# Hybrid decoder layer on one core: the first three heads of cross attention's first half in written order on all engines

## The chip, the core and the metric

The kernel runs on one core of a Trainium2 chip. The metric is device time in microseconds (us). The core has a matrix engine (TensorE, PE in the profile), three engines for the rest (VectorE is DVE, ScalarE is ACT, GpSimd is POOL), each with an instruction queue of its own that is worked off in order, and a queue (SyncE, SP) that issues the transfers between the main memory and the core's buffers. Engines wait for each other through semaphores. Matrix products are gathered in eight banks of PSUM.

## The reference

One decoder layer, 1024 tokens of 1024 columns, in float32: two mixers in parallel (mLSTM and forgetting attention), then cross attention over 256 memory tokens in four heads of 256 columns, then an MLP with squared ReLU, each behind an RMS norm.

```python
def cross_attention(h, memn, w_q, w_kv, w_o):
    q = (h @ w_q).reshape(B, S, X_HEADS, X_DH)
    k, v = jnp.split(memn @ w_kv, 2, axis=-1)
    ...
    s = jnp.einsum('bqhd,bmhd->bhqm', q, k) * (X_DH ** -0.5)
    p = jax.nn.softmax(s, axis=-1)
    o = jnp.einsum('bhqm,bmhd->bqhd', p, v).reshape(B, S, D)
    return o @ w_o
```

The change lies in the queries, scores, softmax and values of this function.

## The kernel before

Every float32 operand is split into a high half (rounded to the engine's fast format, ScalarE, line 134 or 137) and a low half (what is left over, VectorE, line 135 or 138). `mm3` multiplies them in three matmuls, lines 186 (low weight by high operand), 187 (high by low) and 188 (high by high). What is called a cut below is such a split.

The 1024 tokens are worked in two halves of 512. For the **first half** of cross attention each head has two query tiles (`n` = 0 to 7 over the four heads). A tile takes a weight load of 512 KB (`weights`, two buffers `wr` for the raw weights and three pairs `wh`, `wl` for the halves), eight times three matmuls into a PSUM bank (`mm` for the even tile, `m2` for the odd one; each exists once; the profile calls the second `m`), and a cut that also evicts it, into `r_b`, `r_c` or `r_p`, `r_a`, `r_y`. `cross_head` then does, for one head: loads of keys and values; scores of four token tiles into two of three `sc` banks; the maximum (line 1289, times `rcol` in 1291) on VectorE, four exponentials on ScalarE (1293), a reciprocal (1294), four scalings (1296); a `yield`; eight transposes on PE (1301, the turns) into two `tp` banks and the cut of these (`r_d`, `r_e`); two value products, one for each 128 columns of the head, each gathered in the one `ov` bank and cut into `oh`, `ol` (both `act` tiles).

For the **second half** the queries are made another way: `query_blocks` multiplies blocks of the weights, added and subtracted beforehand (`left_query`: SP loads two raw tiles at once, VectorE line 1223 and GpSimd lines 1339 and 1227 add, cuts follow), by seven combinations of the normed tokens (`R`, made by `right_side(k)` for k = 0 to 3, tiles also called `act`). `right_side(k)` loads two tiles into the two `r_f` buffers, scales them (ScalarE, 1177), cuts three pieces, and then three times subtracts on GpSimd (1339) in place and cuts the result. A product of `query_blocks` sums over all four k.

`row_second(1)` makes the second half's norm factors: `rsqrt_sums` sums columns on PE (234) into `ov`, VectorE, GpSimd (a power, 204) and VectorE again make `rcol`; `to_row` turns it on PE (249), copies it (ScalarE, 250) and sends it by way of main memory into `row`.

What sets the order: the kernel is recorded in the order of the Python code, and then a scheduler with its own picture of times orders each engine's queue, by dependencies and by what it takes to be ready. Only inside `in_order()` are the instructions of PE, ScalarE, VectorE and GpSimd (not SP) tied to the written order; instructions written outside such a block may still be placed between them. In the kernel before, the loop over the four heads of the first half lies outside any such block, so the scheduler lays products of later tiles and of `query_blocks` between a head's steps.

Of the kernel before, what the change touches and what calls it, by code (L numbers as in the profile page):

```python
# [21 lines left out]
KT = D // P  # L22
# [22 lines left out]
def hybrid_layer(ctx: ExitStack, tc: tile.TileContext, a: dict, out: bass.AP):  # L45
# [123 lines left out]
    def weights(src, n=1024):  # L169
        return weight_parts(weight_load(src, n))  # L170
# [992 lines left out]
    def cut_right(c, k, x):  # L1163
        split(R[c][0][:, k], R[c][1][:, k], x)

    fourth = []

    def right_side(k):
        if not fourth:
            for c in (("11", "21"), ("t1", "t2"), ("22", "t3")):  # L1170
                right_room(*c)
            fourth.append(w4((P, 4, 256)))
        x, y = w2("f"), w2("f")
        for t, n in ((x, k), (y, 4 + k)):
            with tc.issue_after(mix_done[0].ins):
                load(t, x1d[1, :, n])
            s.activation(t, t, AF.Copy, scale=ln_x(n))
# [12 lines left out]
    def q_room(kk):  # L1190
        return [rotate(*tags).bitcast(F32R) for tags in ((("b",), ("c",)), (("p",), ("a", "y")))[kk]]

    def query_whole(hd):
        q = []
        for kk in range(2):
            t = q_room(kk)
            for _, _, ps in proj(weights(a["w_xq"][2 * hd + kk]), [h2], 1, order=[(0, 0)], into=ps_tile(("mm", "m2")[kk])):
                split(*t, ps, 1.0 / 16.0)
            q.append(t)
        return q  # L1200

    x_jobs = [(hd, i) for hd in range(XH) for i in X_ORDER]
    x_first = {}
# [69 lines left out]
    def cross_head(hd, hf, q, oh, ol):  # L1273
        kx, vx = w4(dt=F32R), w4(dt=F32R)
        with tc.issue_after(mix_done[0].ins):
            load(kx.bitcast(F32), kxd[hd].rearrange("p e k c -> p (e k c)"))
            load(vx.bitcast(F32), vxd[hd].rearrange("p e m c -> p (e m c)"))
        kx, vx = (t.rearrange("p (e k c) -> p e k c", e=2, k=2) for t in (kx, vx))
        vx_parts = (vx[:, 0], vx[:, 1])
        pts = [(w2("d", dt=F32R), w2("e", dt=F32R)) for _ in range(2)]  # L1280
        pr = z4()[:, :T].rearrange("p (i c) -> p i c", i=4)
        den, rden, mxc = col("den", 4), col("rden", 4), col("mx", 4)
        sps = [sc().rearrange("p (i c) -> p i c", i=2) for _ in range(2)]
        for i in range(4):
            sp = sps[i // 2]
            for kk in range(2):
                mm3(sp[:, i % 2], both(q[kk], lambda z: z[:, i * P : (i + 1) * P]), (kx[:, 0, kk], kx[:, 1, kk]), kk == 0, kk == 1)
            if i % 2:
                v.tensor_reduce(out=mxc[:, i - 1 : i + 1], in_=sp, axis=mybir.AxisListType.X, op=ALU.max, negate=True)

                v.tensor_tensor(out=mxc[:, i - 1 : i + 1], in0=mxc[:, i - 1 : i + 1], in1=rcol[:, 4 * hf + i - 1 : 4 * hf + i + 1], op=ALU.mult)
        for i in range(4):
            s.activation(pr[:, i], sps[i // 2][:, i % 2], AF.Exp, bias=mxc[:, i : i + 1], scale=rcol[:, 4 * hf + i : 4 * hf + i + 1], accum_out=den[:, i : i + 1])
        v.reciprocal(rden, den)
        for i in range(4):
            s.activation(pr[:, i], pr[:, i], AF.Copy, scale=rden[:, i : i + 1])
        yield
        for m in range(2):
            ps = tp()
            for i in range(4):  # L1300
                nc.tensor.transpose(ps[:, i * P : (i + 1) * P], pr[:, i, m * P : (m + 1) * P], ident)
# [36 lines left out]
    def sub(out_, x, y, by=v):  # L1338
        by.tensor_tensor(out=out_, in0=x, in1=y, op=ALU.subtract)
# [108 lines left out]
    os_ = []  # L1448
    whole = act(), act()
    os_.append([Rows(enumerate(t[:, n] for n in range(KT))) for t in whole])  # L1450
    for hd in range(XH):
        q = query_whole(hd)
        right_side(hd)
        if hd == XH - 1:
            last_room = right_room("t4")
            for k in range(4):
                cut_right("t4", k, fourth[0][:, k])
            for _ in range(2):
                left_query(*x_prep.pop(0))
# [388 lines left out]
```

## Time and profile before

| | |
|---|---|
| time, median of 3 runs | 1511.72 us (1510.87 to 1512.04) |
| span of the profiled execution | 1509.2 us |
| instructions | 22358 |
| TensorE's mean granted clock | 0.997 |
| the stage of the change in the trace | from about 628 us |

The span runs from the first to the last instruction of the profiled execution; the timed runs are some 2.5 us longer, with what lies around it. The profile has no other time of that execution. A row of a timeline gives the start in us from the span's start, the duration in us, the engine, the line, the operation, the tile written and the tiles read (without buffer numbers), the shape, the count of equal instructions that follow each other, and in brackets the idle time of the engine before it with what ended that. PE's matmuls overlap: the next starts before the last has ended, so a PE that is busy all the time can still run slower than it could, and the distance from start to start is what counts.

### The profile page before, as it was taken

What the parts mean: (1) busy time and instruction counts of PE and PEld (TensorE: products, weight loads), DVE (VectorE), ACT (ScalarE), POOL (GpSimd) and SP (SyncE); (2) the same over time, 40 slices, a digit from 0 to 9 for tenths busy, and PEclk for the clock granted to TensorE, in tenths of its full rate; (3) what the DMA queues carried; (4) which work ended last, traced back from release to release, by engine and by line L of the source; (5) the groups of instructions that cost most, each with busy time, mean ns of one, the idle gap of its engine ahead of it and who ended that gap; (6) DMA issues with size and microseconds to landing.
All of it is one profiled execution on the core that took longest, in us unless ns stands there. A gap on an engine that the chain in (4) does not pass through costs nothing.

```text
span 1509.2 us, 22358 instructions
## 1 busy us (share of the span) xinstructions
PE 1493.0 (99%) x7806; PEld 1263.7 (84%) x7806; DVE 1122.7 (74%) x1803; ACT 757.7 (50%) x1440; POOL 528.7 (35%) x545
## 2 busy tenths in 40 slices
PE   9999999999999999999999999999999999999997
PEld 9988888889899888788988878888888888888887
DVE  7766676664788875667767899989996678787765
ACT  7324343334688764566654467566664521122134
POOL 1003030414365441623300044454544365553312
PEclk9999999999999999999999999999999999999999
DMA  6322333435777877853354447676678677776623
GB/s 243 115 79 95 98 108 126 132 129 153 247 261 256 284 248 246 271 169 126 128 182 159 147 155 279 235 261 248 217 273 292 264 279 279 279 272 251 247 88 112
DMA packets 124276, 303.04 MB, mean 201 GB/s; under 512 B 13810, under 2 KB 28460, under 8 KB 117252
## 3 DMA queue, kind: packets, MB, share of 16 engines
q1 hardware_dynamic: 124164, 301.62, 57.3%
q8 instruction: 61, 1.00, 0.3%
q14 instruction: 51, 0.42, 0.1%
HBM read 202.75 MB, written 98.82 MB: 200 GB/s over the span
## 4 chain that ended last, share of the span: by engine, by line
PE 90%; DMA 4%; DVE 3%; ACT 1%; issue 1%; POOL 1%; POOLq 0%; DVEq 0%; SPq 0%; ACTq 0%
PE tp L186 8%; PE tp L187 8%; PE tp L188 8%; PE sc L186 6%; PE sc L188 6%; PE sc L187 6%; PE mm L186 5%; PE m L188 5%; PE m L186 5%; PE m L187 5%; PE mm L188 5%; PE mm L187 5%; PE ov L801 2%; PE ov L186 2%; PE ov L187 2%; PE ov L188 2%
## 5 line engine op out<-in xcount | busy, mean ns | idle before, releaser
L186 PE MATMUL tp<-act,wl 128*128 128x512 f32 (+1 forms) x440 | 172.6, 392 | 0.0
L187 PE MATMUL tp<-act,wh 128*128 128x512 f32 (+1 forms) x440 | 172.1, 391 | 0.0
L188 PE MATMUL tp<-act,wh 128*128 128x512 f32 (+1 forms) x440 | 171.8, 392 | 0.0
L135 DVE TENSOR_TENSOR wl<-wr,wh 128x1024 fp32r<-128x1024 f32 (+2 forms) x99 | 131.4, 1327 | 27.0 <-ACT wh L134 26.7
L134 ACT ACTIVATE wh<-wr 128x1024 fp32r<-128x1024 f32 (+2 forms) x99 | 99.8, 1008 | 85.7 <-PE tp L188 32.7
L186 PE MATMUL mm<-act,wl 128*128 128x512 f32 (+1 forms) x332 | 124.8, 376 | 2.6 <-DVE r_c L138 2.1
L188 PE MATMUL mm<-act,wh 128*128 128x512 f32 (+1 forms) x332 | 124.1, 374 | 0.0
L187 PE MATMUL mm<-act,wh 128*128 128x512 f32 (+1 forms) x332 | 123.8, 373 | 0.0
L186 PE MATMUL m<-act,wl 128*128 128x512 f32 (+1 forms) x308 | 113.8, 369 | 0.6 <-DVE wl L135 0.6
L188 PE MATMUL m<-act,wh 128*128 128x512 f32 (+1 forms) x308 | 113.8, 369 | 0.0
L187 PE MATMUL m<-act,wh 128*128 128x512 f32 (+1 forms) x308 | 113.7, 369 | 0.0
L188 PE MATMUL sc<-act,wh 128*128 128x512 f32 (+1 forms) x280 | 105.6, 377 | 0.0
L187 PE MATMUL sc<-act,wh 128*128 128x512 f32 (+1 forms) x280 | 105.6, 377 | 0.0
L186 PE MATMUL sc<-act,wl 128*128 128x512 f32 (+1 forms) x280 | 105.6, 377 | 0.0
L1612 POOL TENSOR_TENSOR z<-wr 128x256 f32<-128x256 f32 x56 | 52.9, 966 | 131.8 <-DMA wr<-w_ff2q 126.7
L188 PEld LDWEIGHTS tp<-act,wh 128*128 128x128 f32 x440 | 82.7, 188 | 19.0
L186 PEld LDWEIGHTS tp<-act,wl 128*128 128x128 f32 x440 | 82.7, 188 | 18.5
L187 PEld LDWEIGHTS tp<-act,wh 128*128 128x128 f32 x440 | 82.7, 188 | 18.2
L134 ACT ACTIVATE wh<-z 128x1024 fp32r<-128x1024 f32 (+1 forms) x54 | 55.5, 1027 | 81.8 <-POOL z L1612 62.3
L135 DVE TENSOR_TENSOR wl<-z,wh 128x1024 fp32r<-128x1024 f32 (+1 forms) x54 | 77.7, 1439 | 11.4 <-ACT wh L134 11.4
L134 ACT ACTIVATE w<-wr 128x768 fp32r<-128x768 f32 (+3 forms) x35 | 28.0, 801 | 107.4 <-PE tp L186 33.0
L186 PEld LDWEIGHTS mm<-act,wl 128*128 128x128 f32 x332 | 62.7, 189 | 14.2 <-DVE r_c L138 2.6
(734 smaller groups left out, 4387.2 us busy)
## 6 DMA issues: line engine op xcount, KB each, us to landing
act<-right SPq DMA_DIRECT2D x49, 1024.0 KB
right<-w SPq DMA_DIRECT2D x56, 256.0 KB
wr<-w_ff2q SPq DMA_DIRECT2D x28, 512.0 KB
right<-r_d SPq DMA_DIRECT2D x49, 256.0 KB
right<-r_e SPq DMA_DIRECT2D x49, 256.0 KB
act<-fqk SPq DMA_DIRECT2D x48, 256.0 KB
wr<-w_in SPq DMA_DIRECT2D x20, 512.0 KB
wr<-w_ff SPq DMA_DIRECT2D x20, 512.0 KB
```

What stands on the lines that cost most here:

```text
L134: s.activation(hi, src, AF.Copy)
L135: return v.tensor_tensor(out=lo, in0=src, in1=hi.bitcast(F32), op=ALU.subtract)
L186: nc.tensor.matmul(ps, w[1], x[0], start=first, stop=False, skip_group_check=more)
L187: nc.tensor.matmul(ps, w[0], x[1], start=False, stop=False, skip_group_check=more)
L188: nc.tensor.matmul(ps, w[0], x[0], start=False, stop=last, skip_group_check=more)
L801: nc.tensor.matmul(self.ov[:, c0:], self.fv[:, self.j], t[:, c0:], start=self.j == 0 and t is self.p[1], stop=self.last and t is self.p[0])
L1612: g.tensor_tensor(out=o, in0=x, in1=y, op=op)
```

## The change

The loop over the first three heads is put inside `in_order()`. The query tiles are made one at a time by three small functions (weights, product, cut), and a head's steps stand so: the cut of the next head's first tile, scores and softmax, the product of the next head's second tile, the first part of `right_steps`, the turns, the cut of that tile, the product of the tile after it, the rest of `right_steps`, another weight cut, the values. `row_second(1)` moves from behind head 0 to between the first two products and the third. Head 3 stays outside, and its two query tiles are made by then. `right_side` becomes a generator with one `yield`, and `cross_head` gets a second `yield` between turns and values.

```diff
+    def right_steps(k):
...
         cut_right("11", k, x1)
         cut_right("21", k, y1)
         cut_right("22", k, y2)
+        yield
         sub(x1, x2, x1, g)
         cut_right("t1", k, x1)
...
-    def query_whole(hd):
...
+    w_query, p_query, queries = {}, {}, {}
+
+    def query_weights(n):
+        if n < KT:
+            w_query[n] = weights(a["w_xq"][n])
+
+    def query_product(n):
+        if n < KT:
+            ((_, _, p_query[n]),) = proj(w_query.pop(n), [h2], 1, order=[(0, 0)], into=ps_tile(("mm", "m2")[n % 2]))
+
+    def query_cut(n):
+        if n < KT:
+            queries[n] = q_room(n % 2)
+            split(*queries[n], p_query.pop(n), 1.0 / 16.0)
...
             split(*pts[m], ps)
+        yield
         for kk in range(2):
...
-    for hd in range(XH):
-        q = query_whole(hd)
-        right_side(hd)
-        if hd == XH - 1:
...
-        for _ in cross_head(hd, 0, q, *os_[0]):
-            pass
-        if hd == 0:
-            row_second(1)
+    with in_order():
+        for n in range(2):
+            query_weights(n)
+        query_product(0)
+        query_weights(2)
+        query_cut(0)
+        query_product(1)
+        row_second(1)
+        query_weights(3)
+        query_cut(1)
+        query_product(2)
+        for hd in range(XH - 1):
+            query_cut(2 * hd + 2)
+            query_weights(2 * hd + 4)
+            steps = cross_head(hd, 0, [queries.pop(2 * hd + kk) for kk in range(2)], *os_[0])
+            next(steps)
+            query_product(2 * hd + 3)
+            side = right_steps(hd)
+            next(side)
+            next(steps)
+            query_cut(2 * hd + 3)
+            query_product(2 * hd + 4)
+            next(side, None)
+            query_weights(2 * hd + 5)
+            for _ in steps:
+                pass
+    right_side(XH - 1)
...
+    for _ in cross_head(XH - 1, 0, [queries.pop(2 * XH - 2 + kk) for kk in range(2)], *os_[0]):
+        pass
```

How the queues stand at three places, before and after. Line numbers of the changed kernel are some 4 to 11 higher (1181 for 1177, 1307 for 1296, 1312 for 1301, 1351 for 1339).

First, ScalarE where head 0's queries are evicted (`mm_7130` and `m_1357` are the first two tiles; `act_7192` to `act_7194` hold the right side). Before:

```order
L222 ACTIVATE r_c_7106<-r_p_7102 128x512
L134 ACTIVATE act_7192<-r_f_7197 128x256
L134 ACTIVATE act_7194<-r_f_7197 128x256
L134 ACTIVATE act_7193<-r_f_7196 128x256
L134 ACTIVATE act_7194<-r_f_7196 128x256
L137 ACTIVATE r_b_7122<-mm_7130 128x512
L134 ACTIVATE wh_7358<-wr_7356 128x1024
```

After (`mm_7134`, `m_1358` and `mm_7222` are the first three tiles, `ov_7207` the turned norm factors):

```order
L222 ACTIVATE r_c_7106<-r_p_7102 128x512
L137 ACTIVATE r_b_7165<-mm_7134 128x512
L250 ACTIVATE row<-ov_7207 8x128
L134 ACTIVATE wh_7214<-wr_7212 128x1024
L137 ACTIVATE r_p_7218<-m_1358_7169 128x512
L137 ACTIVATE r_b_7247<-mm_7222 128x512
L134 ACTIVATE wh_7253<-wr_7251 128x1024
```

The right side's cuts, which wait for GpSimd, have moved from ahead of the first query eviction to behind head 0's softmax.

Second, PE where head 0's values are made (`ov_7283` and `ov_7292` before, `ov_7408` and `ov_7417` after). Before, the first value product:

```order
L187 MATMUL sc_7424<-w_1399_7411,r_b_7319 128x256
L186 MATMUL ov_7283<-r_d_7222,w_1365_7219 128x512
L188 MATMUL sc_7424<-w_1399_7411,r_b_7319 128x256
...
L187 MATMUL ov_7283<-r_e_7225,w_1365_7219 128x512
L188 MATMUL ov_7283<-r_d_7224,w_1365_7219 128x512
L186 MATMUL m_1426_7537<-act_6784,wl_7534 128x512
```

After, from the last matmul of a query product on:

```order
L188 MATMUL mm_7367<-act_6784,wh_7253 128x512
L186 MATMUL ov_7408<-r_d_7261,w_1376_7258 128x512
...
L187 MATMUL ov_7408<-r_e_7264,w_1376_7258 128x512
L188 MATMUL ov_7408<-r_d_7263,w_1376_7258 128x512
L186 MATMUL ov_7417<-r_d_7261,w_1376_7258 128x512
...
L188 MATMUL ov_7417<-r_d_7263,w_1376_7258 128x512
L186 MATMUL sc_7448<-w_1409_7436,r_c_7248 128x256
```

Before, head 1's scores and a query product of 24 matmuls and more stood between the two value products; now the second follows the first in the same bank.

Third, head 2 between its softmax and its values. ScalarE before (`z_1435` holds the probabilities, `tp_7637` the first turns, `act_7761` the fourth right tile):

```order
L1296 ACTIVATE z_1435_7594<-z_1435_7594,c_rden_7596 128x256 x4
L134 ACTIVATE act_7761<-w_1361_7195 128x256 x4
L137 ACTIVATE r_p_7704<-m_1456_7712 128x512
L134 ACTIVATE wh_7879<-wr_7772 128x1024
...
L134 ACTIVATE r_d_7590<-tp_7637 128x512
```

ScalarE after (`z_1442` the probabilities, `r_f_7681` and `r_f_7682` the right side's slice 2, `tp_7693` and `tp_7700` the turns):

```order
L1307 ACTIVATE z_1442_7613<-z_1442_7613,c_rden_7615 128x256 x4
L1181 ACTIVATE r_f_7681<-r_f_7681,vec 128x512
L1181 ACTIVATE r_f_7682<-r_f_7682,vec 128x512
L134 ACTIVATE act_7761<-w_1391_7336 128x256 x2
L134 ACTIVATE wh_7879<-wr_7772 128x1024
L134 ACTIVATE act_7333<-r_f_7681 128x256
L134 ACTIVATE act_7333<-r_f_7682 128x256
L134 ACTIVATE act_7335<-r_f_7682 128x256
L134 ACTIVATE r_d_7609<-tp_7693 128x512
L134 ACTIVATE r_d_7611<-tp_7700 128x512
L137 ACTIVATE r_p_7707<-m_1448_7656 128x512
```

PE after, from the second tile of turns on (`mm_7883` is the first block of `query_blocks`, its matmuls here read slice 2; `sc_7802` are head 3's scores):

```order
L1312 MATMUL tp_7700<-ident,z_1442_7613 128x128 x4
L186 MATMUL mm_7883<-act_7333,wl_7778 128x256
L186 MATMUL ov_7721<-r_d_7609,w_1437_7606 128x512
L187 MATMUL mm_7883<-act_7333,wh_7777 128x256
L188 MATMUL mm_7883<-act_7333,wh_7777 128x256
L187 MATMUL ov_7721<-r_e_7610,w_1437_7606 128x512
...
L187 MATMUL ov_7721<-r_e_7612,w_1437_7606 128x512
L188 MATMUL ov_7721<-r_d_7611,w_1437_7606 128x512
L186 MATMUL sc_7802<-w_1467_7790,r_y_7708 128x256
```

Before, the right side had been cut long ahead of this place and other products stood around the turns; now slice 2 of the right side is cut between softmax and turns, and on PE only pieces that read this slice or the turns stand there.

More of the change, by code (lines that the diff above doesn't have):

```diff
@@ L1450, in hybrid_layer @@
     os_.append([Rows(enumerate(t[:, n] for n in range(KT))) for t in whole])
-    for hd in range(XH):
-        q = query_whole(hd)
-        right_side(hd)
-        if hd == XH - 1:
[L1455 to L1459, printed above, removed]
-        for _ in cross_head(hd, 0, q, *os_[0]):
-            pass
-        if hd == 0:
-            row_second(1)
+    with in_order():
[25 more added lines that the diff above has]
+    right_side(XH - 1)
+    last_room = right_room("t4")
+    for k in range(4):
+        cut_right("t4", k, fourth[0][:, k])
+    for _ in range(2):
+        left_query(*x_prep.pop(0))
+    for _ in cross_head(XH - 1, 0, [queries.pop(2 * XH - 2 + kk) for kk in range(2)], *os_[0]):
+        pass
     oh, ol = Rows(), Rows()
```

8 lines of the change are left out of this document (1 added, 7 removed).

## The prediction

> **What bounds the kernel now.** I read the page first: the busy shares and the chain of waits.
>
> ```profile
> span 1509.2 us, 22358 instructions
> PE 1493.0 (99%) x7806; PEld 1263.7 (84%) x7806; DVE 1122.7 (74%) x1803; ACT 757.7 (50%) x1440; POOL 528.7 (35%) x545
> PE 90%; DMA 4%; DVE 3%; ACT 1%; issue 1%; POOL 1%; POOLq 0%; DVEq 0%; SPq 0%; ACTq 0%
> ```
>
> TensorE (PE) is busy for 99% of the span and is 90% of the chain that ended last. So the change, which moves no arithmetic, can only win the time in which PE waits or runs slowly, and whatever new wait it gives PE is paid in full. Next come the stretches of the edited stage (us; then busy time and instructions of PE, PEld, DVE, ACT and POOL; granted clock; DMA share; GB/s), and PE's own timeline at the two places where it is not dense.
>
> ```profile
> 628.16:639.20 11.04, 11.04 (x49) 8.92 (x49) 5.57 (x10) 4.89 (x9) 7.05 (x7) 1.00 0.85 281
> 639.20:642.46 3.26, 1.12 (x5) 0.63 (x4) 2.94 (x4) 2.71 (x7) 2.03 (x3) 1.00 0.63 250
> 642.46:645.88 3.42, 3.42 (x11) 2.65 (x10) 2.59 (x4) 2.10 (x4) 0.00 (x0) 0.50 0.87 287
> 645.88:704.60 58.72, 58.72 (x346) 50.70 (x346) 38.02 (x71) 39.23 (x95) 16.95 (x18) 1.00 0.43 139
> ```
>
> ```profile
> 638.97 0.40 PE L187 MATMUL m<-act,wh 128*128 128x512 f32 x1
> 639.20 0.39 PE L188 MATMUL m<-act,wh 128*128 128x512 f32 x1
> 641.74 0.50 PE L186 MATMUL mm<-act,wl 128*128 128x512 f32 x1 [2.14 <-DVE r_c L138]
> 642.60 0.63 PE L186 MATMUL mm<-act,wl 128*128 128x512 f32 x1
> 643.03 0.63 PE L187 MATMUL mm<-act,wh 128*128 128x512 f32 x1
> ...
> 704.53 0.28 PE L187 MATMUL sc<-act,wh 128*128 128x256 f32 x1
> 704.65 0.28 PE L188 MATMUL sc<-act,wh 128*128 128x256 f32 x1
> 705.34 0.38 PE L186 MATMUL mm<-act,wl 128*128 128x256 f32 x1 [0.42 <-DVE wl L135]
> ```
>
> Starts follow each other by 0.23 us at 512 columns and by 0.12 at 256, so a query tile's product (24 matmuls) is 5.6 us of PE, a head's scores (24 of 256) 2.86, one value product (6 of 512) 1.4.
>
> **What goes.** After 639.20 the next start is 2.54 us later instead of 0.23: 2.3 lost. For the next 3.42 us the clock is 0.50 and the pitch 0.43: eight matmuls lose about 0.2 each, 1.65 with the edges. At 704.65 another 0.57 is lost. Together 4.5 us. The first wait is the one that the new order on ScalarE removes: the query eviction stood behind cuts that waited for GpSimd.
>
> ```profile
> 639.74 0.42 ACT L134 ACTIVATE act<-r_f 128x256 fp32r<-128x256 f32 x1 [0.53 <-POOL r_f L1339]
> 640.18 0.60 ACT L137 ACTIVATE r_b<-mm 128x512 fp32r<-128x512 f32 x1
> 641.01 0.68 DVE L138 SCALAR_TENSOR_TENSOR r_c<-mm,r_b 128x512 fp32r<-128x512 f32 x1
> ```
>
> The tile had been finished since about 634; now its eviction runs during the next product and is free, as that product covers it by over 4 us.
>
> **What comes, a: the row of the second norm.** `row_second(1)` now stands between products 1 and 2 on PE: sums, a chain over VectorE and GpSimd, then a transpose that reads its result. Nothing on PE may pass. The kernel's end has the same chain:
>
> ```profile
> 1499.04 1.31 PE L1748 MATMUL sc<-ones,r_b 128*128 128x1 f32 x8 [0.49 <-POOL r_b L226]
> 1500.63 0.71 POOL L1750 TENSOR_TENSOR c_y<-c_var,half 128x2 f32<-128x2 f32 x1 [1.64 <-DVE c_var L1749]
> 1501.97 0.71 PE L213 MATMUL mm<-ident,c_r 128*128 128x128 f32 x4 [1.62 <-DVE c_r L1754]
> ...
> 633.28 1.02 POOL L204 TENSOR_TENSOR c_y<-c_var,half 128x4 f32<-128x4 f32 x1
> ```
>
> PE idles 1.62 there; four columns instead of two make GpSimd 0.3 longer: 1.9, I take **2.0**. Behind the transpose on PE stands product 2, then head 0's scores, so all of the stage moves. The sums and the transpose themselves are not new, they ran later.
>
> **b: one bank for two value products.** The `ov` bank exists once. In heads 0 and 1 the second product now follows the first, so PE waits for the whole split. In the profile other matmuls stood between.
>
> ```profile
> 696.71 0.39 PE L188 MATMUL ov<-r_d,w 128*128 128x512 f32 x1
> 697.13 0.60 ACT L134 ACTIVATE act<-ov 128x512 fp32r<-128x512 f32 x1 [2.37 <-PE ov L188]
> 698.35 0.68 DVE L135 TENSOR_TENSOR act<-ov,act 128x512 fp32r<-128x512 f32 x1
> ```
>
> End of PE to ScalarE 0.03, then 0.60, hop 0.04, 0.68, hop 0.05: idle 1.40, and 1.57 from start to start. The split also queues behind the right side's three cuts and a weight cut, written ahead of it. Counted from the end of the turns, PE is through the first value product after 5.6 + 1.4 = 7.0. In head 0 that queue ends at 6.7 on ScalarE and 7.9 on VectorE, so the low half of the split is ready at 8.6: **1.6**. In head 1, where the turns come late (c), VectorE is through at 8.8 and the low half at 9.4: **2.4**. Behind it stand the second value product and the next head's scores.
>
> **c: head 1's turns.** The loads are in no written order, but SP issues them one after the other, and each waits for its buffer there. Weights 3 to 7 and the keys of heads 1 and 2 are issued over 5 us before their use, so I cost them at nothing; ahead of that cover only a load slower by 5 us would show. One load is late. Ahead of the scaling of the probabilities ScalarE now holds a cut of the second half's first weight tile, and VectorE an add on it. That load needs the buffer of tile 6, whose cut ends 3.4 us after the scores' start, and loads take 3.5:
>
> ```profile
> 691.45 0.33 SPq L174 DMA_DIRECT2D wr<-w_xq  x1
> 695.01 0.70 DVE L1223 TENSOR_TENSOR wr<-wr 128x512 f32<-128x512 f32 x1 [2.61 <-DMA wr<-w_xq]
> 658.89 1.69 ACT L1296 ACTIVATE z<-z,c_rden 128x256 f32<-128x256 f32 x4
> 728.82 1.03 PE L1301 MATMUL tp<-ident,z 128*128 128x128 f32 x8
> ```
>
> Landing at 7.0, add and reciprocal to 7.95, scaling to 9.65; PE, with scores and one product, is there at 8.46, and its eight turns end at 10.25 instead of 9.36: **0.9**. In head 0 the chain has half a us to spare.
>
> **d: head 2, turns to values.** In heads 0 and 1 a query product lies between turns and values; head 2 has none (no tile 8). After the last scaling, ScalarE holds two gains, two cuts of the fourth tile, a weight cut and three right cuts before it evicts the turns; VectorE the same halves.
>
> ```profile
> L1177 ACT ACTIVATE r_f<-r_f,vec 128x512 f32<-128x512 f32 x8 | 5.8, 724 | 9.8 <-DMA r_f<-x1d 9.8
> L134 ACT ACTIVATE wh<-wr 128x1024 fp32r<-128x1024 f32 x15 | 15.9, 1058 | 2.5 <-DMA wr<-w_xq 1.2 <-POOL wr L1227 1.2
> 656.14 1.22 DVE L135 TENSOR_TENSOR wl<-wr,wh 128x1024 fp32r<-128x1024 f32 x1 [0.26 <-ACT wh L134]
> 660.49 1.02 ACT L134 ACTIVATE act<-r_f 128x256 fp32r<-128x256 f32 x3
> 682.89 1.28 DVE L135 TENSOR_TENSOR r_e<-tp,r_d 128x512 fp32r<-128x512 f32 x2
> ```
>
> From the last scaling: gains 1.26, cuts 0.65, weight high half 1.05 (to 2.95), VectorE's low half 1.22 (4.2), three low cuts (5.3), two turn halves 1.28 (6.55), the last query cut (7.1), which head 3's scores need. PE ends the turns at 0.5 and has nine matmuls (1.76) in these 6.6 us: **4.9**.
>
> **e: head 3 and the first query block.** The last slice of the right side loads into a buffer that head 2's third sum frees, at about 10.0 on the same clock (three GpSimd steps of 0.85 with the cuts between).
>
> ```profile
> 664.71 0.85 POOL L1339 TENSOR_TENSOR r_f<-r_f,r_f 128x256 f32<-128x256 f32 x1 [1.55 <-DVE act L135]
> 666.41 0.80 SPq L1176 DMA_DIRECT2D r_f<-x1d  x2
> 669.83 0.73 ACT L1177 ACTIVATE r_f<-r_f,vec 128x512 f32<-128x512 f32 x1 [3.81 <-DMA r_f<-x1d]
> L1293 ACT ACTIVATE z<-sc,c_mx,rcol 128x256 f32<-128x256 f32 x20 | 11.1, 560 | 4.1 <-DVE c_var L198 3.3 <-DVE c_mx L1291 0.8
> ```
>
> Issue to use is 3.3, so 13.3. Then ScalarE alone has 8.6 us (two gains, four exponentials, six cuts of 0.31, one of 0.52, one eviction, four scalings, a turn), and with VectorE's half head 3's values start at 22.3. PE has 5.05 us of scores, block parts and values ready from 7.1 on (18 score matmuls 2.15, twelve of the block 1.45, a value product 1.4) and 2.7 more in pieces behind the cuts (three times three of the block, the eight turns, half a value product): 15.2 less 7.75 is **7.4**. No product of the block can step in, since each sums over all four slices of the right side and the last slice is the late one. From there on the block has all it needs, and I count nothing.
>
> **The clock.** Each wait long enough may cost a stretch at half clock, 1.65. In the rows above an idle 2.14 did it; this one of 1.07 did not:
>
> ```profile
> 385.44 0.50 PE L734 MATMUL sc<-act 128*128 128x512 f32 x1 [1.07 <-ACT act L756]
> 385.44:392.00 6.56, 6.56 (x52) 6.39 (x53) 5.39 (x18) 4.15 (x12) 3.67 (x6) 1.00 1.01 358
> ```
>
> Five new waits (a, b of head 1, d, two in e) lie near or over 2: none to five stretches, 0 to 8.3; I take two, **3.3**, as the waits of d and e are partly empty time where a slow clock harms nothing.
>
> The Trainium skill, page "TensorE: Matmul & The Clock Gate", section "HAM oscillation — how this bites in real kernels", sets the rule at no idle gap over about 3.4 us. The row of 2.14 goes against it as a bound on one gap. By the page only d and e could slow the clock, and the sum would be 1.65 lower.
>
> **The sum.** 2.0 + 1.6 + 0.9 + 2.4 + 4.9 + 7.4 + 3.3 = 22.5, less 4.5: 18.0 us over the profiled span, 1527.2. The median shown, 1511.72, is 2.5 above the span; I carry that over: 1529.7, say **1529**, 1.1% slower. Moving values ahead adds no PE work: all these matmuls ran before, later.
>
> **Unknowns.** d and e rest on chains of ten and more steps; if loads land a us earlier and half of d and e is covered, 6.2 go, without slow clocks 3.3 more: 1520. All five stretches and VectorE's weight half at its crowded mean (1.34 for 1.22) give 1536; a block that starves after that, 1538.
>
> **Rivals.**
> - *Only the order's two fixed waits count.* a and twice b, 5.2, against 4.5 gone, perhaps one slow stretch: 1512.4 to 1514.1, **1513**. It needs ScalarE in heads 2 and 3 to keep up; for it, ACT is busy 39 of 58.7 us in the fourth stretch above. Against it, the last head has no product to hide 6.6 us of queue. Chance 0.12, two thirds of it inside 0.2%.
> - *Faster.* The starved places fill with block products that need only the slices already cut, and the bank is handed over within another product's tail. 4.5 goes and 1.0 comes: **1508**. It decides at a to e together under 1.5 us. The fixed orders of PE at a and b alone speak against it. Chance 0.04.
> - *The clock as the bound.* PE works in pieces from head 1 to the first block, stays at 0.50 for most of it and pays over 9: **1540**. For it, one wait of 2.14 was enough; against it, dense stretches in between. Chance 0.06.
>
> My forecast keeps 0.78. Slower by over 0.2% (3 us, about what a measurement can tell from no change): 0.78 + 0.06 + 0.04 = 0.88; within: 0.08; faster: 0.04. The range 1513 to 1538 takes in the first rival's middle.
>
> **What the profile after would show.** No wait of `mm` on the first query cut; about 2.0 idle before the transpose of `rcol`; `ov` waiting for VectorE's `act` half twice, about 1.4 and 2.2; PE waiting before head 2's `ov` and head 3's scores, some 5 in all; PE before the block's `mm` and `m` on ScalarE's right cuts, some 7; several stretches of clock 0.50. I am wrong if PE stays dense from head 2's turns on, or if the loads of the right side's last slice start before head 2's cuts end.

## The result and the profile after

| | before | after |
|---|---|---|
| time, median of 4 runs each | 1511.3 us (1509.7 to 1512.0) | 1536.5 us (1534.0 to 1537.7) |
| span of the profiled execution | 1509.2 us | 1534.8 us |
| mean granted clock | 0.997 | 0.991 |

The ratio is 1.0161, with a 95% interval of 1.0148 to 1.0173: slower by 25 us. The forecast was slower, 1529, in a range of 1513 to 1538. The direction and the range held; the size was 7.5 us short, and the measured time lies 1.5 us below the upper end of a range 25 us wide. Where the record has both, a timed run lies some 1.7 us above its own span; the 2.5 carried over in the prediction is that and some 0.8 by which the profiled execution was faster than the median.

First the page of the changed kernel: span, busy time of PE, and the chain that ended last.

```profile
span 1534.8 us, 22367 instructions
PE 1503.5 (98%) x7806; PEld 1268.3 (83%) x7806; DVE 1125.4 (73%) x1803; ACT 758.2 (49%) x1440; POOL 528.1 (34%) x545
PE 89%; DVE 4%; DMA 3%; ACT 2%; issue 1%; POOL 1%; SPq 0%; POOLq 0%; DVEq 0%; ACTq 0%
```

PE has the same 7806 matmuls, and its busy time is 10 us longer although the work is the same. Some 4.5 us of that is the slow clock, which stretches each matmul (6.0 us lost to it in this stage, 1.5 before, by the measure below): it stood at 0.50 for 27.1 us of the span, against 10.0 before. The other part is waiting too: a matmul ahead of a wait is shown busy for its whole 0.39 us, where the next would have started after 0.23. The remaining 15 of the 25 us is idle time. Where it lies, the stretches of the stage show (columns as in the prediction: length, then busy time of PE, PEld, DVE, ACT and POOL, granted clock, DMA share, GB/s).

```profile
627.00:650.00 23.00, 20.97 (x92) 16.84 (x91) 9.26 (x16) 5.54 (x9) 9.16 (x7) 0.93 0.72 243
650.00:690.00 40.00, 35.55 (x180) 28.77 (x179) 22.61 (x39) 24.68 (x56) 6.28 (x8) 1.00 0.35 117
690.00:704.90 14.90, 13.04 (x75) 10.80 (x74) 7.87 (x10) 6.65 (x16) 6.00 (x4) 1.00 0.49 146
704.90:715.80 10.90, 7.02 (x25) 5.51 (x26) 7.02 (x13) 7.60 (x17) 3.15 (x4) 0.69 0.17 50
715.80:735.00 19.20, 15.07 (x77) 12.53 (x77) 12.06 (x23) 12.60 (x30) 7.95 (x8) 0.73 0.26 82
735.00:770.00 35.00, 34.53 (x279) 33.32 (x279) 29.70 (x48) 20.63 (x49) 13.38 (x9) 1.00 0.36 112
```

PE is short of work from 650 on, worst between head 2's turns (705) and head 3's values (730). In those 30 us no engine is full: VectorE is busy for 19 us and ScalarE for 20. They wait for each other and for loads. Behind 735 PE is dense again. What PE waited for, longest first (total, times, longest):

```profile
PE ov L186 <- DVE act L135: 4.2, 2, 2.3
PE mm L186 <- ACT act L134: 3.5, 2, 2.3
PE m L186 <- ACT act L134: 2.1, 1, 2.1
PE ov L249 <- DVE rcol L208: 2.0, 1, 2.0
...
PE sc L186 <- ACT z L1304: 1.8, 2, 1.4
```

The first row is b, the second and third belong to d and e, the fourth is a. The last, ahead of head 2's turns, is a wait that the prediction did not have. The wait of `mm` for the first query cut is gone, as forecast.

To give every kernel below the same measure, I sum over PE's starts in the trace the distance to the next start less the pitch of that shape (0.233 us at 512 columns, 0.118 at 256, 0.108 for a turn). What is left is PE's **loss**. From 627 to 770 it was 4.7 us before and 29.7 after, and the spans differ by 25.6. A single distance of more than 0.25 over the pitch counts as a wait; what is lost in shorter ones inside a stretch of clock 0.50 counts as slow clock.

### The profile page after: what moved, and what is told of

It is laid out like the page before. It is cut to its first block, busy times and chain, and to the rows that moved or that the text cites. A ratio compares the mean times of both kernels' runs of the same rounds, so it can differ in the third digit from the quotient of the medians.

```text
span 1534.8 us, 22367 instructions
## 1 busy us (share of the span) xinstructions
PE 1503.5 (98%) x7806; PEld 1268.3 (83%) x7806; DVE 1125.4 (73%) x1803; ACT 758.2 (49%) x1440; POOL 528.1 (34%) x545
## 4 chain that ended last, share of the span: by engine, by line
PE 89%; DVE 4%; DMA 3%; ACT 2%; issue 1%; POOL 1%; SPq 0%; POOLq 0%; DVEq 0%; ACTq 0%
PE tp L186 8%; PE tp L187 8%; PE tp L188 8%; PE sc L186 6%; PE sc L188 6%; PE sc L187 6%; PE mm L186 5%; PE m L187 5%; PE m L186 5%; PE mm L188 5%; PE m L188 5%; PE mm L187 5%; PE ov L801 2%; PE ov L186 2%; PE ov L187 2%; PE ov L188 2%
## 5 line engine op out<-in xcount | busy, mean ns | idle before, releaser
L1645 POOL TENSOR_TENSOR z<-wr 128x256 f32<-128x256 f32 x56 | 49.5, 904 | 131.2 <-DMA wr<-w_ff2q 110.5
```

The source lines that it names most:

```text
L1645: g.tensor_tensor(out=o, in0=x, in1=y, op=op)
```

## The experiments

All times are medians in us. Losses are in us from 627 to 650 (first query tiles and the norm's row), 650 to 690 (heads 0 and 1) and 690 to 770 (head 2 to the first block). The last column is how long the clock stood at 0.50 between 627 and 770. Each ratio is to runs of the kernel before made beside that kernel; its median in those groups lay between 1510.9 and 1512.5, so the ratios compare better than the medians. The intervals of e5_pad, e6_left_behind and e9_pad_head2 overlap that of the changed kernel, and that of e1_row_split touches it.

| kernel | median | ratio to before, 95% | loss 627–650 | 650–690 | 690–770 | at 0.50 |
|---|---|---|---|---|---|---|
| before | 1511.3 | | 4.1 | 0.3 | 0.3 | 3.4 |
| after, the changed kernel | 1536.5 | 1.0148 to 1.0173 | 4.0 | 5.9 | 19.8 | 20.5 |
| e1_row_split | 1530.8 | 1.0118 to 1.0149 | 0.2 | 6.6 | 16.5 | 17.1 |
| e2_two_banks | 1526.2 | 1.0089 to 1.0119 | 3.8 | 0.1 | 14.9 | 17.1 |
| e3_two_heads | 1526.6 | 1.0085 to 1.0119 | 3.8 | 3.2 | 12.8 | 10.2 |
| e4_last_slice | 1530.5 | 1.0114 to 1.0144 | 2.3 | 6.5 | 13.6 | 10.2 |
| e5_pad | 1534.8 | 1.0133 to 1.0160 | 0.6 | 7.0 | 18.9 | 20.5 |
| e6_left_behind | 1538.8 | 1.0162 to 1.0189 | 2.3 | 5.5 | 23.5 | 17.1 |
| e7_first_tiles | 1512.5 | 0.9993 to 1.0010 | 0.1 | 2.0 | 2.1 | 0 |
| e9_pad_head2 | 1534.4 | 1.0125 to 1.0157 | 3.8 | 6.4 | 14.3 | 10.2 |
| e10_keys_first | 1511.6 | 0.9984 to 1.0002 | 0.0 | 0.8 | 2.3 | 0 |
| e11_three_edits | 1522.8 | 1.0060 to 1.0088 | 0.2 | 0.1 | 15.7 | 10.2 |
| e12_two_slices | 1519.1 | 1.0034 to 1.0062 | 0.2 | 8.0 | 3.4 | 6.8 |
| e13_turns_first | 1531.1 | 1.0108 to 1.0136 | 3.9 | 6.9 | 14.8 | 20.5 |

Ahead of 627 the program is the same in all of them, and there the loss differed by up to 2.4 from one execution to another. So a difference of one or two us between two totals says little; the losses by place say more. One caution holds for all of them: what stands outside the written order is placed anew by the scheduler in each kernel, so an edit can also act through a place that it doesn't touch.

**The norm's row (a).** `e1_row_split` leaves the sums where they are and moves the transpose behind the third product:

```diff
         query_product(1)
-        row_second(1)
+        rsqrt_sums(x1_accs[1], rcol[:, 4:8], 4)
         query_weights(3)
         query_cut(1)
         query_product(2)
+        to_row(row, rcol, 8, rowd[2:3])
```

> The changed kernel (1536.5), but of the second norm's row only the sums stay between query products 1 and 2; the transpose and what follows it stand behind product 2. Theory W (PE waits in the written order, and half clock follows where PE is thin): the wait of 2.0 before the transpose goes, because product 2 (5.6 us) covers the chain, and with it the half-clock window that came 1.4 us after it; the changed kernel lost 4.0 us between 627 and 650, so 1532.5. Rival C (the clock falls for a reason of its own, not for this wait): only the 2.0 goes, 1534.5, and a row of clock 0.50 stays before 650. Rival M (the wait moves on to the next thing late): no change, 1536.5.

Measured: 1530.8. From 627 to 650 the loss fell from 4.0 to 0.2, so 3.8 of the 4.0 that W named, and the half clock there is gone. The rest of the gain lies elsewhere: the stretch behind 690 lost 3.3 less, with waits that now fall differently. `e5_pad` keeps the wait and fills it:

```diff
         query_product(1)
-        row_second(1)
+        rsqrt_sums(x1_accs[1], rcol[:, 4:8], 4)
+        pad = tp()
+        for n in range(8):
+            nc.tensor.matmul(pad, h2[0][:, n, :P], h2[0][:, n], start=n == 0, stop=n == 7)
+        to_row(row, rcol, 8, rowd[2:3])
```

> The changed kernel, but eight matmuls of 512 columns, whose result nothing reads, are put on PE between the second norm's sums and its transpose (8 x 0.23 = 1.9 us of work in the idle 2.03 us); nothing is left out. Theory W with the clock as a result of PE's thin stretch: the chain takes as long as before, so no idle time is won or lost, but the half-clock window after it goes: 1536.5 - 1.8 = 1534.7. Rival C (the clock falls for a reason of its own): the half-clock row stays, 1536.5. If the added work itself delays PE: 1537 to 1538.

Measured: 1534.8, as W had it, though the interval doesn't tell it from the changed kernel. The window behind the filled wait runs at full clock, as it should if the half clock was a result of the idle PE:

```profile
639.99:643.40 3.41, 3.34 (x20) 2.61 (x19) 0.65 (x4) 0.11 (x1) 1.02 (x1) 1.00 0.13 54
643.40:646.82 3.42, 3.42 (x16) 2.74 (x15) 1.83 (x2) 1.58 (x3) 0.00 (x0) 1.00 0.28 107
```

The table shows a smaller loss in this place (0.6) than the time does, because the eight added matmuls, 1.9 us, count as work. That the total came out at W's figure is in part chance: another window of half clock came at 667 (7.0 lost in heads 0 and 1 in place of 5.9), and 0.9 less was lost behind 690. One execution doesn't prove the cause either, since `e4_last_slice` and `e6_left_behind` have the wait unfilled and yet no half clock behind it; the last section counts the windows of all executions.

**One bank for two value products (b).**

```diff
-            ov = ov_()
+            ov = tp() if kk and hf == 0 and hd < XH - 1 else ov_()
```

> The changed kernel, but the second value product of heads 0 to 2 goes into a bank of the turns (tp) in place of the one ov bank. Theory W: the two waits of an ov product for VectorE's act half go (2.06 and 2.50 us lost in heads 0 and 1, none in head 2, where block pieces lay between): 1536.5 - 4.5 = 1532.0. Rival M (the cuts on ScalarE and VectorE are what is late, and the wait moves to the next turns or scores): half or less is won, 1534.3 to 1536.5.

Measured: 1526.2. Heads 0 and 1 lose 0.1 in place of 5.9, so b and c together are gone and nothing moved to the next turns. The edit removes b; c went because the scheduler placed the left query's add otherwise. In the changed kernel it stands ahead of the reciprocal in head 1, so that the scaling and the turns wait for its load:

```profile
677.05 0.69 DVE L1234 TENSOR_TENSOR wr<-wr 128x512 f32<-128x512 f32 x1 [2.07 <-DMA wr<-w_xq]
677.66 0.17 DVE L1305 RECIPROCAL c_rden<-c_den 128x4 f32<-128x4 f32 x1
```

With two banks it stands behind the reciprocal:

```profile
675.17 0.18 DVE L1305 RECIPROCAL c_rden<-c_den 128x4 f32<-128x4 f32 x1 [1.63 <-ACT z L1304]
676.38 0.69 DVE L1234 TENSOR_TENSOR wr<-wr 128x512 f32<-128x512 f32 x1 [1.03 <-DMA wr<-w_xq]
```

The stretch from 690 also lost 4.9 less, which no theory named. The wait for the exponentials ahead of head 2's turns (1.8 in the list above) is not among this kernel's waits; the reasons of the rest aren't separated.

**Head 2's order.** `e3_two_heads` lets the written order end with head 1, and writes head 2 as head 3 is written, outside:

```diff
-        for hd in range(XH - 1):
+        for hd in range(XH - 2):
...
+    query_cut(2 * XH - 2)
+    right_side(XH - 2)
+    for _ in cross_head(XH - 2, 0, [queries.pop(2 * XH - 4 + kk) for kk in range(2)], *os_[0]):
+        pass
+    query_product(2 * XH - 1)
+    query_cut(2 * XH - 1)
     right_side(XH - 1)
```

> The changed kernel, but only heads 0 and 1 stand in the written order; head 2 is left to the scheduler like head 3. Between 690 and 733 the changed kernel loses 19.4 us, the kernel before 0.6 at the like place. Theory W (it is head 2's written order, without a query product between turns and values, that starves PE): most of it goes, 1517 to 1524, I take 1520. Rival L (the right side's last slice is late already from heads 0 and 1, and the first query block waits for it whoever orders head 2): the 7 us of the block's waits and two or three half-clock windows stay, 1527 to 1530.

Measured: 1526.6, just under the lower end of L. Of the 19.8 behind 690, 7.0 went, 12.8 stayed. Heads 0 and 1 lost 2.7 less as well, which neither theory named. By this run head 2's own written order is about a third of the loss behind 690; the rest is there too when only heads 0 and 1 are ordered. The next kernels ask where it comes from.

**The right side's last slice (e).**

```diff
-        x, y = w2("f"), w2("f")
+        if k == XH - 1:
+            t = z4()
+            x, y = t[:, :512], t[:, 512:1024]
+        else:
+            x, y = w2("f"), w2("f")
```

> The changed kernel, but the last slice of the right side loads into a buffer of another kind (of the probabilities' pool), so that the load need not wait for head 2's third sum. Theory W as I had it for e (load issued at 715.4, used at 718.2, and then a long queue on ScalarE): load and gains are done before head 2's cuts, the cuts for the block stand some 3 us earlier; with one half-clock window less 1531 to 1533, I take 1532. Rival Q (ScalarE's and VectorE's queue of cuts is the bound, the load is hidden in it): under 1 us, 1535.5 to 1536.5.

Measured: 1530.5. Behind 690 the loss fell by 6.2, more than W had. But 1.7 of what the profiled execution gained isn't the edit's: the wait a is as long as in the changed kernel, yet no half clock followed it (see the last section). That execution was also the fastest of the four, 1.8 below their median. `e13_turns_first` puts the cuts of the turns ahead of the right side's:

```diff
-            next(side)
             next(steps)
+            next(side)
             query_cut(2 * hd + 3)
```

> The changed kernel, but in each head of the written order the turns and their cuts stand ahead of the first three cuts of the right side, not behind them. Theory W as I had it for d (head 2's values wait for the cuts of the turns, and those stand behind gains and cuts of 2.9 us on ScalarE): the values start some 3 us earlier after the turns; the right side comes 1.1 us later and gives a part back in the block: 1534.5. Rival Q (whatever stands first, the block then waits for the queue's end): 1536.5. In heads 0 and 1, where a product covers, nothing changes by either.

Measured: 1531.1, better than W. In the changed kernel PE's timeline at d was:

```profile
708.37 0.39 PE L186 MATMUL mm<-act,wl 128*128 128x256 f32 x1 [2.32 <-ACT act L134]
709.47 0.80 PE L186 MATMUL ov<-r_d,w 128*128 128x512 f32 x1 [0.70 <-ACT r_d L134]
...
711.48 0.79 PE L187 MATMUL ov<-r_e,w 128*128 128x512 f32 x1 [0.79 <-DVE r_e L135]
```

and here:

```profile
705.65 0.51 PE L186 MATMUL ov<-r_d,w 128*128 128x512 f32 x1 [0.87 <-ACT r_d L134]
707.07 0.50 PE L187 MATMUL ov<-r_e,w 128*128 128x512 f32 x1 [0.91 <-DVE r_e L135]
```

The queue of right cuts ahead of the turns' cuts was what d waited for: 2.3 and more are gone, and the loss behind 690 is 5.0 smaller. Heads 0 and 1 pay 1.0 more there; their second value products wait 2.7 and 2.6 for the first one's split, and I take it, without a run that shows it, that this split now stands closer behind the right cuts. The edits of e1, e2 and e4 together:

> The changed kernel with the edits of e1 (row split), e2 (two banks) and e4 (last slice in a buffer of its own) together. From 627 to 770 the changed kernel lost 29.7 us against its pitch; e1 took 3.8 of it before 650, e2 took 5.8 between 650 and 690 and 4.9 after, e4 took 6.2 after 690. Theory W (the waits are separate places in the order, so the edits add up): 29.7 - 3.8 - 5.8 - 4.9 - 6.2 = 9, so about 1516. Rival Q (what comes after 690 is one queue of cuts on ScalarE and VectorE, and e2 and e4 win the same time there): 1536.5 - 3.8 - 5.8 - 6.2 = 1520.7.

Measured: 1522.8, nearer to Q but 2 above it. Up to 690 the edits of e1 and e2 hold (0.3 lost in all), but behind 690 15.7 remain, more than e2 or e4 alone had. They do not add up. The longest waits left there are for a right cut (the first block) and for the cut of a turn, so I read what is left as one chain of cuts, in which an edit that frees one step meets the next. `e12_two_slices` tests that and takes the work away from there (the edits of e1 and e2 and the buffer for the second slices are left out here):

```diff
-            side = right_steps(hd)
-            next(side)
+            side, side2 = (right_steps(2 * hd + e) if hd < 2 else iter(()) for e in range(2))
+            next(side, None)
             next(steps)
             query_cut(2 * hd + 3)
             query_product(2 * hd + 4)
             next(side, None)
+            next(side2, None)
             query_weights(2 * hd + 5)
             for _ in steps:
                 pass
-    right_side(XH - 1)
+            next(side2, None)
```

> The changed kernel with e1's row split and e2's two banks, and with two slices of the right side in each of heads 0 and 1 (the second of each in a buffer of the probabilities' pool), none in head 2 and none behind it. Theory W (after 690 PE waits because the last two slices are cut where no query product lies between turns and values, and the block needs the last one): heads 0 and 1 have 11 us of query products each to cover 3.5 us more of ScalarE, so some 3 are lost there, and head 2 with head 3 and the block loses 3 where e11_three_edits lost 15.7: 1522.8 - 15.7 + 6 = 1513. Rival Q (the cuts are work that ScalarE and VectorE can't do in time wherever it is put): the loss moves to heads 1 and 2's turns and stays over 12, 1519 to 1523.

Measured: 1519.1, in Q's range and 6 above W. Each theory was right in one half. Behind 690 the loss is 3.4, W's 3, with the clock at 1.00 throughout:

```profile
690.00:704.90 14.90, 13.09 (x84) 11.63 (x83) 12.58 (x18) 8.96 (x23) 8.52 (x7) 1.00 0.39 141
704.90:715.80 10.90, 9.56 (x71) 8.77 (x70) 7.91 (x12) 6.48 (x13) 2.62 (x3) 1.00 0.32 98
715.80:735.00 19.20, 19.20 (x161) 18.88 (x160) 17.11 (x32) 16.08 (x40) 8.68 (x6) 1.00 0.37 116
```

So the two late slices, without a query product beside them, are what starved head 2, head 3 and the block. But heads 0 and 1 lost 8.0, not 3, and nearly all of it is one wait before head 1's turns with the slow clock behind it, where Q had the loss move to (PE, then ScalarE and VectorE ahead of it):

```profile
678.18 1.28 PE L1316 MATMUL tp<-ident,z 128*128 128x128 f32 x3 [4.64 <-ACT z L1311]
674.29 0.57 ACT L1308 ACTIVATE z<-sc,c_mx,rcol 128x256 f32<-128x256 f32 x1 [2.15 <-DVE c_mx L1306]
676.80 0.69 DVE L1238 TENSOR_TENSOR wr<-wr 128x512 f32<-128x512 f32 x1 [1.81 <-DMA wr<-w_xq]
677.41 0.17 DVE L1309 RECIPROCAL c_rden<-c_den 128x4 f32<-128x4 f32 x1
```

PE's product had its last start at 673.15, and the exponentials began only at 674.29, because on VectorE the cuts of the second slice stood ahead of the maximum. That is the greater part; the left query's add, waiting for its load, held the reciprocal for some 0.8 more. Room beside a query product is limited: of the 12.3 us won behind 690, 7.9 were lost again in heads 0 and 1.

**Loads at the head of a queue (c).** `e6_left_behind` writes the left query cuts, the last slice and the fourth tile into the ordered block behind head 2 (they are indented into it; nothing else changes):

```diff
-    right_side(XH - 1)
+        right_side(XH - 1)
...
-    for _ in range(2):
-        left_query(*x_prep.pop(0))
+        for _ in range(2):
+            left_query(*x_prep.pop(0))
```

> The changed kernel, but the right side's last slice, its fourth tile and the first two groups of the left query cuts also stand in the written order, behind head 2, so that the scheduler can no longer put the left cuts into heads 1 and 2. Theory W (each fixed place is paid, and the work put behind head 2 is what PE waits for next): the 0.9 before head 1's turns and the 1.9 before head 2's go, but the block then starts behind all the cuts: slower, 1538 to 1543, I take 1540. Rival S (the scheduler's left cuts, which wait on a load at the head of ScalarE's and VectorE's queues, are the fault): 1536.5 - 2.8 = 1533.7.

Measured: 1538.8. W's total, though the interval doesn't tell it from the changed kernel, and not for W's reason alone. Beside the block's waits for left cuts, PE has one of head 3's scores for their keys, whose load comes late here:

```profile
PE sc L186 <- DMA w<-kxd: 3.6, 1, 3.6
```

What the run does show is that both waits for a left cut are gone: PE has no wait before head 1's or head 2's turns. In the changed kernel's timeline ScalarE stood idle for 5.2 us between the two value splits of head 1, because the scheduler had put a left query cut there, and VectorE's maximum came late behind the low half (ScalarE, VectorE and PE one after the other):

```profile
693.54 1.06 ACT L134 ACTIVATE wh<-wr 128x1024 fp32r<-128x1024 f32 x1 [5.23 <-DMA wr<-w_xq]
```

```profile
697.68 2.05 DVE L135 TENSOR_TENSOR wl<-wr,wh 128x1024 fp32r<-128x1024 f32 x1
699.65 1.24 DVE L1302 TENSOR_TENSOR c_mx<-c_mx,rcol 128x2 f32<-128x2 f32 x1
```

```profile
702.24 0.38 PE L186 MATMUL sc<-w,r_c 128*128 128x256 f32 x1 [1.45 <-ACT z L1304]
703.33 0.39 PE L186 MATMUL sc<-act,wl 128*128 128x256 f32 x1 [0.35 <-ACT z L1304]
```

**The clock in head 2.**

```diff
             query_product(2 * hd + 4)
+            if hd == XH - 2:
+                pad = ov_()
+                for n in range(12):
+                    nc.tensor.matmul(pad, h2[0][:, n % 8, :P], h2[0][:, n % 8], start=n == 0, stop=n == 11)
             next(side, None)
```

> The changed kernel, but twelve matmuls of 512 columns, whose result nothing reads, stand on PE between head 2's turns and values (12 x 0.23 = 2.8 us of work, into the bank of the values, in a place where PE idles 2.3 us and then works in pieces); nothing is left out. Theory W with the clock as a result of thin stretches: the values start at the same time or up to 0.5 later, but the half-clock window from 709 to 716 goes, and some 18 matmuls in it no longer lose 0.2 each, in part hidden by waits: 1536.5 - 1.5 = 1535.0. Rival C (the clock costs nothing there, as PE waits anyhow, or falls without regard to PE's work): 1536.5 to 1539, the added work showing as far as it isn't hidden.

Measured: 1534.4; W had 1535.0. 2.8 us of useless matmuls made the kernel no slower; its median is 2 us lower, but the interval overlaps that of the changed kernel, and the runs spread from 1530.7 to 1536.1, so a gain isn't shown. The clock stood at 0.50 for 10.2 us of the stage in place of 20.5, but not just where W had it: a window from 712.0 to 715.4 stayed slow, one at 691 came, and the three from 722.6 on went. In the table's loss the 2.8 counts as work.

**A version without the new waits.** `e7_first_tiles` orders only the start (against the kernel before; the loop's body, which now skips what is done already, is left out):

```diff
+    with in_order():
...
+        query_product(0)
+        query_weights(2)
+        query_cut(0)
+        query_product(1)
+        query_weights(3)
+        query_cut(1)
+        query_product(2)
+        right_side(0)
     for hd in range(XH):
...
```

> The written order only over the first query tiles (products 0 to 2, the cuts of tiles 0 and 1 and the right side's first slice behind them); all heads and the norm's row are left to the scheduler as in the kernel before (1511.3). Theory W: the kernel before's wait of 2.3 for the first query cut and the half clock of 1.65 behind it go and no fixed wait comes: 1511.3 - 4.0 = 1507.3. Rival M (the wait goes to the next thing late on ScalarE): 1510 to 1511.5. Rival L (the right side starts later by 4 us, and the block waits for its last slice): 1513 to 1516.

Measured: 1512.5, ratio 1.0002, so not W. The old wait and its half clock went (0.1 lost before 650 in place of 4.1), but 2.0 came in heads 0 and 1 and 2.1 behind them, as rival M had it, though not on ScalarE. The largest of them is a load again, the keys of head 0, issued behind the weights of tiles 3 to 6:

```profile
652.80 0.39 PE L186 MATMUL sc<-w,r_c 128*128 128x256 f32 x1 [1.61 <-DMA w<-kxd]
```

`e10_keys_first` writes that load ahead of the block (`keys` holds the two loads that stood in `cross_head`):

```diff
+    early.append(keys(0))
     with in_order():
...
-        kx, vx = w4(dt=F32R), w4(dt=F32R)
+        kx, vx = early.pop() if early else keys(hd)
```

> e7_first_tiles, but the loads of head 0's keys and values are written ahead of the query tiles, so that they are not issued behind the weights of tiles 3 to 6. In e7 (1512.5) head 0's scores waited 1.6 for the keys, and PE's start came 1.8 late. Theory W: that goes and nothing takes its place, 1510.7, 0.1% under the kernel before. Rival M (another load, a weight tile or the first slice of the right side, is late in its place): 1512.5.

Measured: 1511.6, ratio 0.9993 with an interval of 0.9984 to 1.0002. Heads 0 and 1 lose 0.8 in place of e7's 2.0, so the step did what it should. The stage's loss is 3.1 in place of 4.7 before, but 1.6 us are about what the measurement can tell from nothing. No version here is shown to beat the kernel before.

## Why the prediction came out as it did

The table sets the terms of the prediction beside the loss of the changed kernel from 627 to 770, in us.

| term | forecast | measured |
|---|---|---|
| a, the norm's row | 2.0 | 2.2 |
| b, the value bank, heads 0 and 1 | 1.6 + 2.4 | 2.1 + 2.5 |
| c, head 1's turns | 0.9 | 0.9 |
| waits from 690 into head 2's turns | not named | 2.7 |
| d, head 2's turns to values | 4.9 | 5.3 |
| e, head 3 and the first block | 7.4 | 6.4, and 0.8 more up to 770 |
| slow clock | 3.3 | 6.0 |
| small distances | | 1.0 |
| sum (before rounding) | 22.5 | 29.7 |

- **What goes** was right: the wait of `mm` for the first cut is gone, and `e7_first_tiles` lost 0.1 in the place where 4.1 were lost before. Of the 4.5 named as gone, the half clock came back behind the new wait a.
- **a and b** were right in mechanism and nearly in size. `e1_row_split` and `e2_two_banks` remove them, each by its own edit.
- **c** had the right cause, a left query cut that waits for its load at the head of a queue. The step that failed is the sentence on the loads, "I cost them at nothing; ahead of that cover only a load slower by 5 us would show. One load is late." Two were: the same thing happened to the second raw tile, and 2.7 came before head 2's turns. That those cuts cause it, `e6_left_behind` shows: with them out of heads 1 and 2 both waits are gone. In `e2_two_banks` c is gone too, by another place for the add.
- **d and e** were right in sum: 12.3 forecast, 11.7 measured up to 735. The chain of e ran nearly as forecast: counted from the end of head 2's last scaling, the last slice's load was issued at 10.1 (forecast 10.0), used at 12.9 (13.3), and head 3's values began at 23.0 (22.3). In the working, 6.6 less 1.76 is 4.8 and not 4.9, and PE's 5.05 adds up to 5.0; that changes the sum by 0.1. For d the cause is shown by `e13_turns_first`. For e it is shown in part: `e4_last_slice` frees the last slice's load, and `e12_two_slices` leaves 3.4 of everything behind 690 once no slice is cut there. That the two are one chain and not two prices, `e11_three_edits` speaks for, since the gains don't add up. `e3_two_heads` corrects my picture in one point: I put the loss down to head 2's own order, but 12.8 of 19.8 is lost there too when only heads 0 and 1 are ordered. So the agreement of the sum is better than the understanding behind it: by which waits the loss remains with only heads 0 and 1 ordered isn't separated.
- **The clock** is the term that was mis-sized: two stretches were taken, "as the waits of d and e are partly empty time where a slow clock harms nothing", and there were six windows. In the thinner stretches each cost less than in dense work, as that sentence had it, some 0.9 against 1.6 for the one behind a by the same count, but three times as many came. With the second late load this is 5.4 of the 7.2 by which the sum fell short. The range held because its upper end counted five slow stretches that it priced in full; six came, most of them cheaper, and beside them a late load that the range did not have. In part that is luck.
- **The rivals.** Only the two fixed waits (1513): ScalarE in heads 2 and 3 did not keep up, as the argument against it said. Faster (1508): a and b alone were 6.8. The clock as the bound (1540) was nearest in time, but 6.0 of 29.7 is clock; the waits are 22.8.

## What to carry to other kernels

An order that is written out pays at each place where an engine with one instruction at its head stops: a chain that begins and ends on PE needs another product laid into it, two products that share one bank need a second bank, and work that is free beside a product isn't free in the round that has none, nor when twice as much of it is put beside one product. In an order that is only partly fixed, what the scheduler may still put between the fixed instructions stops them, above all a step that waits for a load. When the clock may fall, count the idle time in a window and not the longest gap.

## What the runs showed of the hardware

**The clock is decided window by window, and where a window begins is chance.** In every execution the stretches of clock 0.50, but for the one that runs past the kernel's end, were 3.41 us long or two or three times that, and they began at whole multiples of 3.413 us from each other; the phase differed from one execution to the next. The changed kernel and `e4_last_slice` have the same wait before the norm's transpose:

```profile
642.75 0.27 PE L249 MATMUL ov<-ident,rcol 128*8 128x128 f32 x1 [2.03 <-DVE rcol L208]
```

```profile
641.65 0.27 PE L249 MATMUL ov<-ident,rcol 128*8 128x128 f32 x1 [2.04 <-DVE rcol L208]
```

Cut at the windows of its own clock, the changed kernel reads so:

```profile
637.30:640.71 3.41, 3.41 (x20) 2.84 (x18) 1.65 (x4) 0.00 (x0) 0.70 (x1) 1.00 0.92 363
640.71:644.12 3.41, 1.38 (x8) 1.16 (x8) 0.65 (x4) 1.06 (x2) 1.02 (x1) 1.00 0.00 0
644.12:647.53 3.41, 3.41 (x10) 2.62 (x9) 1.82 (x2) 0.63 (x2) 0.00 (x0) 0.50 0.49 141
```

and `e4_last_slice` so:

```profile
637.31:640.72 3.41, 2.31 (x15) 1.95 (x13) 0.16 (x1) 0.00 (x0) 0.82 (x1) 1.00 0.26 104
640.72:644.13 3.41, 2.48 (x12) 2.04 (x13) 1.41 (x4) 1.69 (x3) 0.20 (x1) 1.00 0.01 1
644.13:647.55 3.42, 3.42 (x17) 2.77 (x16) 0.91 (x2) 0.00 (x0) 0.00 (x0) 1.00 0.73 266
```

In the first the whole wait lies in one window, PE is busy for 1.38 of 3.41, and the next window runs at half clock. In the second the wait lies across two windows with 1.1 and 0.9 idle, and the clock stays. The loss from 627 to 650 was 4.0 and 2.3, so one window of half clock in dense work costs 1.7. In the stage, over all fourteen profiled executions, each of the 25 full-clock windows in which PE idled for 1.83 us or more was followed by half clock; of nine between 1.52 and 1.83, four were; of 492 with 1.52 or less, one was. So the limit lies near half a window in all but that one. It is a share of the window and not one gap: the same idle time cost 1.7 or nothing, by the phase. The one exception is in `e13_turns_first`, where a wait of 2.14 lay across two windows and half clock followed all the same:

```profile
715.04:718.45 3.41, 2.47 (x14) 1.81 (x13) 1.94 (x6) 3.32 (x11) 1.40 (x1) 1.00 0.23 77
718.45:721.87 3.42, 2.15 (x11) 1.25 (x11) 1.43 (x4) 3.42 (x10) 0.17 (x1) 1.00 0.54 156
721.87:725.28 3.41, 3.00 (x8) 1.90 (x8) 2.76 (x6) 1.55 (x5) 2.25 (x3) 0.50 0.00 0
```

PE idled for 0.94 and 1.27 us here. In the second window most of its work was the eight turns; whether these count less than other matmuls no run here separates.

The Trainium skill, page "TensorE: Matmul & The Clock Gate", section "What's actually happening", has a free-running window of 3413 ns, and the traces agree (starts at whole multiples of 3.413 us). A table of that section puts the return to half clock after at least one idle window; here about half a window of idle time was enough.
